# One S5 input chunk and one output-gate chunk share the K tiles on four accumulators

## The chip, the cores and the metric

The kernel runs on one core of a Trainium2 chip. The metric is the device time of one execution in microseconds (us); the median of three runs of the kernel before is 1253.27 us (1252.76 to 1253.33).

## What is computed

One layer of a hybrid block on 272 positions (16 learned meta tokens ahead of 256 tokens) of width 2048, in fp32, cut to what matters here:

```
xn   = rmsnorm(h)                                   # 272 x 2048
q, f, i, g, u = split(xn @ w_in)                    # 5 blocks of 1024 columns
o_hg = hgrn2(q, f, i)  -> per-head rms norm * gain * silu(g)
o_s5 = s5(u)           -> gelu, GLU with w_glu, rms norm
h    = h + concat(o_hg, o_s5) @ w_out
h    = h + conv_ffn(rmsnorm(h))                     # three matrices of 2048 x 5632
out  = rmsnorm(h[16:])
```

`hgrn2` is a gated linear recurrence of 8 heads with a 128x128 state, worked in chunks of 64 positions. `s5` is a diagonal complex state space of 64 groups of 16 channels with 64 states each. The output gate `g` is needed only when a head's output is put together.

## The kernel before, in words

**Matmuls.** Every projection works with fp32 split in two parts: the weights into `whi` (rounded, a ScalarE cast, L160) and `wlo` (the rest, a VectorE subtraction, L82 called by `wsplit`), the activations likewise into `xh` and `xl`. `mm3` issues three matmuls for each tile: high by high (L184), low activations by high weights (L185), high activations by low weights (L186). Weights come in units of 1 MB, that is 8 K tiles (128 rows each) of 256 columns; `wsplit` works them in two halves of 4 K tiles. A half gives 2 column blocks x 4 K tiles x 3 = 24 matmuls. Three buffers of `whi`, three of `wlo` and three raw units are in rotation, so a cast waits for the PE to finish the half three before it.

**Chunks.** `chunk` computes 256 columns of a projection in two PSUM accumulators from 2 units, 96 matmuls. u, f and i chunks are 272 positions wide, q and g chunks 258 (the last 258 positions suffice). The string `ORDER` lists what is written out one after the other: `u0` to `u3` are the S5 input chunks (`do_u`), `h0` to `h3` the f, q and i chunks of two heads each with the recurrence of these heads (`do_h`), `g0` to `g3` the output-gate chunks (`do_g`, then `hg_g` applies silu on ScalarE into `sg` and writes the gate `gs` on VectorE). Then follow the GLU of the S5 half (`gh` in the traces), the output projection (`mh`, `ml` are its activations) and the feed-forward.

**PSUM.** The eight banks are: `pmm`, 3 buffers for accumulators (`acc`); `pbu` 2; `py` 1; `psc` 1; `ptp` 1. A chunk holds two of the three `pmm` buffers until its results are read out, so the next chunk can begin on the third.

**Who sets the order.** The engines' instruction queues run in order. What comes after what on each queue is chosen at build time by a scheduler from priorities (`pri`, a lower number goes first) and its own estimates of durations; the source order is not the queue order.

**Around the start.** While the first chunks run, VectorE also normalises the 16 K tiles of the input (`xn`, L91; `xl`, L82) and works out the S5 coefficients. GpSimd (POOL) raises the S5 poles to powers, a long chain of small products on `pw` and `pt` that starts from a VectorE result (L86). VectorE copies the powers into `ew` (L472) when the chain is through; `cpc` (coefficients, from the scratch tile `sca`) and `W` (the decay weights of the scan) follow. `gs` lies in the same SBUF buffer as `sca`, a pool with one buffer for that tag. `early` holds two raw units loaded ahead of everything else, with part of their `wlo` made by POOL.

**At the end of this stage.** The last head pair's outputs are squared (`sq`), summed per head by the PE (`hps`), VectorE makes the 8 reciprocal roots (`rhv` to `rhy`, `hr`), the PE spreads them over 128 rows (`bps`, L854), VectorE multiplies (`oT`), and `mh`/`ml` of the 8 heads feed the output projection. The same is done for the S5 half (`ssum`, `s5s`, `rfv` to `rfy`, `ysb`), behind the GLU.

Of the kernel before, what the change touches and what calls it, by code (L numbers as in the profile page):

```python
# [9 lines left out]
F32 = mybir.dt.float32  # L10
# [8 lines left out]
T = SEQ + NM  # L19
# [10 lines left out]
T0 = NM - 2  # L30
# [3 lines left out]
NQ = T - T0  # L34
EPS = 1e-6
FLOOR = 1e-6
ORDER = "u0 h0 u1 h1 u2 h2 u3 h3 g0 g1 g2 g3"
U0 = 16
NWARM = 8
NWARM2 = 10  # L40
# [30 lines left out]
def hymba_kernel(ctx: ExitStack, tc: tile.TileContext, x, meta, lb_logits, norm_mix, w_in, hg_norm,  # L71
# [6 lines left out]
    def fact(dst, src, func=AF.Identity, **kw):  # L78
        act.activation(out=dst, in_=src, func=func, **kw)  # L79
# [10 lines left out]
    def stt(dst, a, s, b, op0, op1, **kw):  # L90
        dve.scalar_tensor_tensor(out=dst, in0=a, scalar=s, in1=b, op0=op0, op1=op1, **kw)  # L91
# [41 lines left out]
    def wload(src, parts=1):  # L133
        raw = wrp.tile([128, 2, 1024], F32, tag="raw", name="raw")
        if parts == 2:
            for a in range(2):
                sp.dma_start(out=raw[:, a].rearrange("p (a n) -> p a n", n=src.shape[2]), in_=src[:, 4 * a:4 * a + 4])
            return raw
        sp.dma_start(out=raw.rearrange("p a n -> p (a n)").rearrange("p (a n) -> p a n", n=src.shape[2]), in_=src)
        return raw  # L140

    early = []
    deps = []

    def wunit(src):
        with pri(-4):
            return wsplit(early.pop(0), (dve, pool), 2, deps.pop(0)) if early else wsplit(wload(src))

    def wsplit(raw, eng=(dve, dve), parts=1, dep=None):
        res = []  # L150
        n = 1024 // parts
        for hf in range(2):
            hi = wsp.tile([128, 1024], F32R, tag="whi", name="whi")
            lo = wsp.tile([128, 1024], F32R, tag="wlo", name="wlo")
            if dep is not None and dep[hf] is not None:

                act.copy(out=hi[:, 0:1], in_=dep[hf])
            for i in range(parts):
                c = slice(i * n, (i + 1) * n)
                act.copy(out=hi[:, c], in_=raw[:, hf, c])  # L160
                tt(lo[:, c], raw[:, hf, c], hi[:, c].bitcast(F32), SUB, eng[max(hf, i)])
            res.append((hi, lo))
        return res

    def colunit(w, k, c):
        return w[k * 1024:(k + 1) * 1024, c * 256:(c + 1) * 256].rearrange("(a p) n -> p a n", p=128)

    wpri = [1]

    def mm3(accs, units, rhs, n0, n1):  # L170

        last = len(units) - 1
        for ui, (u, k0) in enumerate(units):
            for hf, (hi, lo) in enumerate(u):
                for m in range(2):
                    for k in range(4):
                        kt = k0 + hf * 4 + k
                        lh = hi[:, k * 256 + m * 128:k * 256 + m * 128 + 128]
                        ll = lo[:, k * 256 + m * 128:k * 256 + m * 128 + 128]
                        first = ui == 0 and hf == 0 and k == 0  # L180
                        end = ui == last and hf == 1 and k == 3
                        xh, xl = rhs(kt)
                        with pri(wpri[0]):
                            pe.matmul(accs[m], lh, xh[:, n0:n1], start=first, stop=False)  # L184
                            pe.matmul(accs[m], lh, xl[:, n0:n1], start=False, stop=False)  # L185
                            pe.matmul(accs[m], ll, xh[:, n0:n1], start=False, stop=end)  # L186

    xh = xnp.tile([128, KD, T], F32R, tag="xh", name="xh")
    xl = xnp.tile([128, KD, T], F32R, tag="xl", name="xl")
# [8 lines left out]
    pmm = pmms.enter_context(tc.tile_pool(name="pmm", bufs=3, space=PSUM))  # L198
# [3 lines left out]
    psc = pa.enter_context(tc.tile_pool(name="psc", bufs=1, space=PSUM))  # L202
# [42 lines left out]
    sp.dma_start(out=crow, in_=conv_w.rearrange("o w (r c) -> (o w r) c", c=128).rearrange("(a p) c -> p a c", p=66))  # L245
    sp.dma_start(out=misc, in_=c_misc)
    sp.dma_start(out=masks, in_=c_masks.rearrange("p (l n) -> p l n", n=64))
    early.append(wload(colunit(w_in, 1, U0)))
    junk = xin.tile([128, D], mybir.dt.bfloat16, name="junk")
    junk2 = xin.tile([128, D], mybir.dt.bfloat16, name="junk2")  # L250

# [91 lines left out]
    def st(nm, p=prm, tag=None):  # L343
        return p.tile([128, NP], F32, tag=tag or nm, name=nm)
# [59 lines left out]
    xr, den, zr, zi, tz = st("xr"), st("den"), st("zr"), st("zi"), st("tz")  # L404
# [99 lines left out]
    k0 = [s5p.tile([128, 128], F32, name=f"k0{i}") for i in range(2)]  # L504
# [53 lines left out]
    def s5_u(j, ps):  # L558
        pv = ps.rearrange("p (k s) -> p s k", s=2)
        act.copy(out=ysb[:, j], in_=pv)  # L560

    def s5_split(j):
        R = s5w.tile([128, 2, TH], F32, tag="R", name="R")
        for q in range(4):
            h = 64 * (q % 2)
            sp.dma_start(out=R[h:h + 64, q // 2], in_=ysb[32 * q:32 * q + 32, j])
        return (R,)
# [104 lines left out]
    def hg_g(h0, accs):  # L672
        sg = hgp.tile([128, 2, NQ], F32, tag="sg", name="sg")
        for m in range(2):
            fact(sg[:, m], accs[m], AF.Sigmoid)
            stt(gs[:, h0 + m], accs[m], vcol[:, V_HG + h0 + m:V_HG + h0 + m + 1], sg[:, m], MUL, MUL)
# [83 lines left out]
    def chunk(w, c, n0=0):  # L760
        units = [(wunit(colunit(w, k, c)), k * 8) for k in range(2)]
        accs = [pmm.tile([128, T - n0], F32, tag="mm", name="acc") for _ in range(2)]
        mm3(accs, units, lambda kt: (xh[:, kt], xl[:, kt]), n0, T)
        return accs


    def do_u(c):
        accs = chunk(w_in, 16 + c)
        with pri(-3):
            for m in range(2):  # L770
                s5_u(2 * c + m, accs[m])
        for m in range(2):
            s5_tile(2 * c + m, *s5_split(2 * c + m), *s5_b(2 * c + m))
# [20 lines left out]
            hg_g(2 * c, accs)  # L794

    for o in ORDER.split():
        {"u": do_u, "h": do_h, "g": do_g}[o[0]](int(o[1]))

    s5ws.close()
    tls = ExitStack()  # L800
# [15 lines left out]
    for c in range(4):  # L816
        u = [(wunit(colunit(w_glu, 0, c)), 0)]
        accs = [pmm.tile([128, NQ], F32, tag="mm", name="acc") for _ in range(2)]
        mm3(accs, u, lambda kt: (gh[:, kt], gl[:, kt]), 0, NQ)
        with pri(-3):  # L820
            for m in range(2):
                j = 2 * c + m
                sg = tlp.tile([128, NQ], F32, tag="sq", name="sgl", bufs=3)
                fact(sg, accs[m], AF.Sigmoid, bias=vcol[:, V_BG + j:V_BG + j + 1])
                yv = ysb[:, j, :, K0:TH]
                tt(yv, yv, sp_view(sg), MUL)
                sq = ssum if j == 0 else tlp.tile([128, NQ], F32, tag="sq", name="sq", bufs=3)
                fact(sp_view(sq), yv, AF.Square)
                if j:
                    tt(ssum, ssum, sq, ADD)  # L830
# [30 lines left out]
    for c in range(8):  # L861
        u = [(wunit(colunit(w_out, 0, c)), 0)]
        accs = [pmm.tile([128, NQ], F32, tag="mm", name="acc") for _ in range(2)]
        mm3(accs, u, mixr, 0, NQ)
        with pri(-3):
            for m in range(2):
                tt(hT[:, 2 * c + m], hT[:, 2 * c + m], accs[m], ADD)
# [23 lines left out]
    for c in range(8):  # L891
        u = [(wunit(colunit(w_out, 1, c)), 8)]
        accs = [pmm.tile([128, NQ], F32, tag="mm", name="acc") for _ in range(2)]
        mm3(accs, u, mixr, 0, NQ)
        for m in range(2):
            kt = 2 * c + m
            g = vcol[:, V_FFN + kt:V_FFN + kt + 1]
# [20 lines left out]
    for c in range(FF // 256):  # L918
        accs = [pf.tile([128, NQ], F32, tag="f", name="ga") for _ in range(2)]
# [12 lines left out]
        accs = [pf.tile([128, NQ], F32, tag="f", name="ua") for _ in range(2)]  # L932
# [15 lines left out]
    for t in range(2):  # L948
        for n in range(4):
            for k in range(4):  # L950
                kt = n * 4 + k
# [20 lines left out]
    for j in range(KF - NT):  # L972
        a = act_split(j)
        u = wunit(w_down[j * 128:(j + 1) * 128, :].rearrange("p (a n) -> p a n", a=2))
# [72 lines left out]
```

## Time and profile before

| | |
|---|---|
| median of three runs | 1253.27 us |
| the profiled execution, device time | 1252.36 us |
| its span | 1250.6 us |
| PE (matmuls) busy | 1226.9 us, 98%, 9299 instructions |
| VectorE (DVE) busy | 873.7 us, 70% |
| ScalarE (ACT) busy | 601.2 us, 48% |
| GpSimd (POOL) busy | 117.0 us, 9% |
| mean granted TensorE clock | 0.994 |
| moved by DMA | 210.82 MB, mean 169 GB/s |

The profile comes from one execution; between its span and its device time lie 1.8 us. Engines are PE, PEld (weight loads, which overlap PE), DVE, ACT, POOL. A row of the timeline gives the start in us, the duration, the engine, the line, the operation, what is written and read, and in brackets how long the engine sat idle before it and whom it waited for. A row of the waits gives the waiting instruction, the releaser, the sum in us, the count and the longest. A row of the windows view gives the length of a stretch, the busy time and instruction count of PE, PEld, DVE, ACT and POOL, the granted clock, the DMA share and GB/s. A row of groups gives a count, the busy time, the mean in ns and the idle time ahead.

### The profile page before, as it was taken

What the parts mean: (1) busy time and instruction counts of PE and PEld (TensorE: products, weight loads), DVE (VectorE), ACT (ScalarE), POOL (GpSimd) and SP (SyncE); (2) the same over time, 40 slices, a digit from 0 to 9 for tenths busy, and PEclk for the clock granted to TensorE, in tenths of its full rate; (3) what the DMA queues carried; (4) which work ended last, traced back from release to release, by engine and by line L of the source; (5) the groups of instructions that cost most, each with busy time, mean ns of one, the idle gap of its engine ahead of it and who ended that gap; (6) DMA issues with size and microseconds to landing.
All of it is one profiled execution on the core that took longest, in us unless ns stands there. A gap on an engine that the chain in (4) does not pass through costs nothing.

```text
span 1250.6 us, 22795 instructions
## 1 busy us (share of the span) xinstructions
PE 1226.9 (98%) x9299; PEld 1151.9 (92%) x9299; DVE 873.7 (70%) x1516; ACT 601.2 (48%) x1042; POOL 117.0 (9%) x165
## 2 busy tenths in 40 slices
PE   7989999999999999999999999999999999999997
PEld 6979898989989999999999999999999988888886
DVE  8989999999748867765665656656656645554554
ACT  5646767574545446343433433433434434444454
POOL 5483132221000000000000000000000000000000
PEclk9989999999999999999999999999999999999999
DMA  8533344243444565565556555555555545555552
GB/s 256 147 122 113 105 144 136 86 134 127 144 135 136 169 201 172 167 203 179 192 172 199 171 196 173 193 178 187 184 181 191 210 166 198 202 188 187 197 205 98
DMA packets 176298, 210.82 MB, mean 169 GB/s; under 512 B 14773, under 2 KB 168880, under 8 KB 170416
## 3 DMA queue, kind: packets, MB, share of 16 engines
q1 hardware_dynamic: 175871, 209.26, 51.1%
q8 instruction: 73, 1.20, 0.4%
q14 instruction: 34, 0.27, 0.1%
q0 software_dynamic: 320, 0.09, 0.0%
HBM read 206.12 MB, written 2.10 MB: 166 GB/s over the span
## 4 chain that ended last, share of the span: by engine, by line
PE 92%; DVE 3%; POOL 2%; issue 1%; DMA 1%; ACT 0%; SPq 0%; DVEq 0%; ACTq 0%; POOLq 0%
PE acc L186 9%; PE acc L184 8%; PE acc L185 8%; PE ua L185 7%; PE ua L184 7%; PE ga L184 7%; PE ua L186 7%; PE ga L186 7%; PE ga L185 7%; PE d L970 6%; PE d L969 6%; PE d L968 6%; PE lps L713 1%; PE bu L600 1%; DVE xn L91 1%
## 5 line engine op out<-in xcount | busy, mean ns | idle before, releaser
L82 DVE TENSOR_TENSOR wlo<-raw,whi 128x1024 fp32r<-128x1024 f32 (+1 forms) x376 | 461.4, 1227 | 320.8 <-ACT whi L160 271.2
L160 ACT CAST whi<-raw 128x1024 fp32r<-128x1024 f32 (+1 forms) x382 | 397.8, 1042 | 519.9 <-PE ga L185 158.3
L184 PE MATMUL ga<-fh,whi 128*128 128x258 f32 x704 | 199.0, 283 | 0.5 <-DVE a L82 0.5
L186 PE MATMUL ga<-fh,wlo 128*128 128x258 f32 x704 | 198.5, 282 | 0.0
L185 PE MATMUL ua<-fl,whi 128*128 128x256 f32 x704 | 198.4, 282 | 0.0
L185 PE MATMUL ga<-fl,whi 128*128 128x258 f32 x704 | 198.1, 281 | 0.0
L186 PE MATMUL ua<-fh,wlo 128*128 128x256 f32 x704 | 197.9, 281 | 0.0
L184 PE MATMUL ua<-fh,whi 128*128 128x256 f32 x704 | 197.9, 281 | 0.0
L186 PE MATMUL acc<-xh,wlo 128*128 128x272 f32 (+1 forms) x640 | 186.7, 294 | 5.0 <-DVE wlo L82 5.0
L185 PE MATMUL acc<-xl,whi 128*128 128x272 f32 (+1 forms) x640 | 186.1, 292 | 3.9 <-DVE xl L82 3.9
L184 PE MATMUL acc<-xh,whi 128*128 128x272 f32 (+1 forms) x640 | 186.4, 294 | 0.4 <-ACT PP L79 0.4
L184 PEld LDWEIGHTS ga<-fh,whi 128*128 128x128 f32 x704 | 133.0, 189 | 0.7 <-DVE a L82 0.7
L185 PEld LDWEIGHTS ga<-fl,whi 128*128 128x128 f32 x704 | 133.5, 190 | 0.0
L184 PEld LDWEIGHTS ua<-fh,whi 128*128 128x128 f32 x704 | 133.1, 189 | 0.0
L186 PEld LDWEIGHTS ua<-fh,wlo 128*128 128x128 f32 x704 | 132.9, 189 | 0.0
L185 PEld LDWEIGHTS ua<-fl,whi 128*128 128x128 f32 x704 | 132.8, 189 | 0.0
L186 PEld LDWEIGHTS ga<-fh,wlo 128*128 128x128 f32 x704 | 132.6, 189 | 0.0
L186 PEld LDWEIGHTS acc<-xh,wlo 128*128 128x128 f32 x640 | 121.4, 190 | 9.4 <-DVE wlo L82 5.6
L185 PEld LDWEIGHTS acc<-xl,whi 128*128 128x128 f32 x640 | 121.6, 190 | 7.5 <-DVE xl L82 4.8
L968 PE MATMUL d<-whi,ah 128*128 128x512 f32 x328 | 127.7, 389 | 0.0
L969 PE MATMUL d<-whi,al 128*128 128x512 f32 x328 | 127.6, 389 | 0.0
L184 PEld LDWEIGHTS acc<-xh,whi 128*128 128x128 f32 x640 | 121.1, 190 | 4.1 <-issue 2.0
(381 smaller groups left out, 1868.1 us busy)
## 6 DMA issues: line engine op xcount, KB each, us to landing
raw<-in_w_ffn_gate SPq DMA_DIRECT2D x44, 1024.0 KB, 5.1
raw<-in_w_ffn_up SPq DMA_DIRECT2D x44, 1024.0 KB, 5.1
raw<-in_w_ffn_down SPq DMA_DIRECT2D x44, 1024.0 KB, 4.8
raw<-in_w_in SPq DMA_DIRECT2D x39, 1024.0 KB, 5.2
raw<-in_w_out SPq DMA_DIRECT2D x16, 1024.0 KB, 5.8
raw<-in_w_glu SPq DMA_DIRECT2D x4, 1024.0 KB, 5.2
x<-in_x SPq DMA_DIRECT2D x4, 512.0 KB, 5.7
out<-ob SPq DMA_DIRECT2D x8, 256.0 KB, 2.7
```

The lines of the kernel that those rows point to most:

```text
L82: eng.tensor_tensor(out=dst, in0=a, in1=b, op=op)
L91: dve.scalar_tensor_tensor(out=dst, in0=a, scalar=s, in1=b, op0=op0, op1=op1, **kw)
L160: act.copy(out=hi[:, c], in_=raw[:, hf, c])
L184: pe.matmul(accs[m], lh, xh[:, n0:n1], start=first, stop=False)
L185: pe.matmul(accs[m], lh, xl[:, n0:n1], start=False, stop=False)
L186: pe.matmul(accs[m], ll, xh[:, n0:n1], start=False, stop=end)
L600: return pe.matmul(bus[i][:, ri], bt[h, 2 * ri + q0 // 2], R[h, q0 // 2], start=True, stop=True)
L713: pe.matmul(ps[:, i], lhs[i], qf[:, 64 * i:64 * (i + 1)], start=True, stop=True)
L968: pe.matmul(dps[t][n], ah[:, tk], hi, start=False, stop=False, skip_group_check=True)
L969: pe.matmul(dps[t][n], al[:, tk], hi, start=False, stop=False, skip_group_check=True)
L970: pe.matmul(dps[t][n], ah[:, tk], lo, start=False, stop=end, skip_group_check=True)
```

## The change

`do_ug` takes the place of `u0` and of `g0`. The first u chunk and the first g chunk are computed together on four accumulators: half a unit of u (24 matmuls), half a unit of g, half a unit of u, and so on through the 16 K tiles. The four accumulators are all three `pmm` buffers and the one `psc` buffer; `gacc` takes the first `pmm` buffer and `psc`. `mm3` gets a `part` that picks the half of a unit. The second of the two early units is now the first g unit, not the second u unit. Then `do_u` goes on with the S5 work, and `hg_g` writes the gate of the first two heads. `ORDER` loses `g0`; `g1 g2 g3` stay at the end. The number of matmuls is the same.

```diff
-ORDER = "u0 h0 u1 h1 u2 h2 u3 h3 g0 g1 g2 g3"
+ORDER = "ug0 h0 u1 h1 u2 h2 u3 h3 g1 g2 g3"
...
-    def mm3(accs, units, rhs, n0, n1):
+    def mm3(accs, units, rhs, n0, n1, part=None):
 
         last = len(units) - 1
-        for ui, (u, k0) in enumerate(units):
+        for ui, (u, k0) in enumerate(units) if part is None else ((part[0], units[part[0]]),):
             for hf, (hi, lo) in enumerate(u):
+                if part is not None and hf != part[1]:
+                    continue
...
-    early.append(wload(colunit(w_in, 1, U0)))
+    early.append(wload(colunit(w_in, 0, 12)))
...
-    def do_u(c):
-        accs = chunk(w_in, 16 + c)
+    def do_ug(c):
+
+        gacc = [pmm.tile([128, NQ], F32, tag="mm", name="acc"), psc.tile([128, NQ], F32, tag="sc", name="acc")]
+        accs = [pmm.tile([128, T], F32, tag="mm", name="acc") for _ in range(2)]
+        xr = lambda kt: (xh[:, kt], xl[:, kt])
+        uu, gu = [None, None], [None, None]
+        for k in range(2):
+            uu[k] = (wunit(colunit(w_in, k, 16 + c)), k * 8)
+            gu[k] = (wunit(colunit(w_in, k, 12 + c)), k * 8)
+            for hf in range(2):
+                mm3(accs, uu, xr, 0, T, part=(k, hf))
+                mm3(gacc, gu, xr, T0, T, part=(k, hf))
+        do_u(c, accs)
+        with pri(-3):
+            hg_g(2 * c, gacc)
+
+    def do_u(c, accs=None):
+        accs = accs or chunk(w_in, 16 + c)
...
-        {"u": do_u, "h": do_h, "g": do_g}[o[0]](int(o[1]))
+        {"u": do_u, "h": do_h, "g": do_g, "ug": do_ug}[o.rstrip("0123456789")](int(o[-1]))
```

How the queues move, at three places. Line numbers of the changed kernel are higher by 2 up to the new function and by 18 behind it.

On PE, the first half of u and the start of the first half of g in the changed kernel (272 wide is u, 258 wide is g):

```order
L188 MATMUL acc<-xh,wlo 128x272
L186 MATMUL acc<-xh,whi 128x272 x2
L186 MATMUL acc<-xh,whi 128x258
L187 MATMUL acc<-xl,whi 128x258
L186 MATMUL acc<-xh,whi 128x258
L187 MATMUL acc<-xl,whi 128x258
L187 MATMUL acc<-xl,whi 128x272
L188 MATMUL acc<-xh,wlo 128x272
```

The matmuls of the two chunks do alternate; in the kernel before all 96 of u stand here without one 258 wide.

On DVE, the queue around the copies of the powers. Before:

```order
L82 TENSOR_TENSOR PP<-PP 128x272
L472 COPY ew<-pw 128x32 x3
L82 TENSOR_TENSOR wlo<-raw,whi 128x1024
L91 SCALAR_TENSOR_TENSOR cpc<-sca 128x32x16
L82 TENSOR_TENSOR qh<-q,PP 128x256
```

Now:

```order
L82 TENSOR_TENSOR sca<-scb,zar 128x512
L474 COPY ew<-pw 128x32 x3
L82 TENSOR_TENSOR wlo<-raw,whi 128x1024
L91 SCALAR_TENSOR_TENSOR cpc<-sca 128x32x16
L91 SCALAR_TENSOR_TENSOR W<-W,pw,tmp 128x2x17 x2
L91 SCALAR_TENSOR_TENSOR gs<-acc,vcol,sg 128x258 x2
L82 TENSOR_TENSOR wlo<-raw,whi 128x1024
L91 SCALAR_TENSOR_TENSOR q<-acc,lbc,sg 128x258 x2
```

The gate `gs` of the first two heads, which reads the g accumulators, stands behind the copies, behind the last reader of `sca` and behind two `W`; the read-out of q (`q<-acc,lbc,sg`) stands behind `gs`, where before it stood ahead of the copies. Ahead of the last VectorE instruction that the POOL chain starts from (L86 `pw`) eight 1024-wide `wlo` now stand where six stood.

On DVE, the reciprocal roots of the last heads at the end of the stage. Before:

```order
L82 TENSOR_TENSOR wlo<-raw,whi 128x1024
L82 TENSOR_TENSOR hr_5309<-rhy,hr_5309 8x258
L82 TENSOR_TENSOR ssum<-ssum,sq 128x258
L82 TENSOR_TENSOR ysb<-ysb,sgl 128x2x129
L82 TENSOR_TENSOR wlo<-raw,whi 128x1024
```

Now:

```order
L82 TENSOR_TENSOR wlo<-raw,whi 128x1024
L82 TENSOR_TENSOR ssum<-ssum,sq 128x258
L82 TENSOR_TENSOR ysb<-ysb,sgl 128x2x129
L82 TENSOR_TENSOR hr_5309<-rhy,hr_5309 8x258
L82 TENSOR_TENSOR ssum<-ssum,sq 128x258
L82 TENSOR_TENSOR oT<-oT,bps 128x258
L82 TENSOR_TENSOR ml<-oT,mh 128x258
L88 TENSOR_SCALAR rfv<-s5s 128x258
```

Counted in halves of units from the start of the program, the nearest `wlo` ahead of `hr` is that of half 87 before, and the PE is still in half 86 when it comes to the first `bps` (L854, now L872). Now it is that of half 91, and on PE the first `bps` stands directly behind the last matmul of half 88, the last of the GLU. From `hr` to the `ml` of the last head DVE has 46 instructions.

## The prediction

> **What bounds the kernel now.** The busy times of the page come first:
>
> ```profile
> PE 1226.9 (98%) x9299; PEld 1151.9 (92%) x9299; DVE 873.7 (70%) x1516; ACT 601.2 (48%) x1042; POOL 117.0 (9%) x165
> ```
>
> PE sets the time nearly everywhere, and the change keeps the number of matmuls. So it can act only through PE's idle time and PE's clock. Where that idle time lies, the waits of PE in the first 100 us and the windows around them tell:
>
> ```profile
> PE acc L186 <- DVE wlo L82: 5.0, 3, 3.6
> PE acc L185 <- DVE xl L82: 3.9, 3, 1.9
> PE dps L685 <- DVE q L91: 0.6, 1, 0.6
> ...
> 18.86:64.39 45.53, 40.76 (x324) 39.15 (x322) 43.06 (x125) 28.30 (x57) 23.44 (x37) 1.00 0.59 170
> 64.39:77.40 13.01, 11.40 (x88) 10.73 (x86) 13.01 (x20) 3.43 (x4) 13.01 (x18) 1.00 0.26 82
> 77.40:80.97 3.57, 0.00 (x0) 0.00 (x0) 2.04 (x6) 0.51 (x3) 3.57 (x6) 0.79 0.00 0
> 80.97:89.72 8.75, 8.75 (x49) 8.25 (x50) 7.85 (x16) 6.70 (x19) 5.75 (x11) 0.50 0.59 183
> 100.00:320.00 220.00, 220.00 (x1975) 200.99 (x1975) 212.15 (x456) 141.85 (x392) 55.65 (x64) 1.00 0.40 122
> ```
>
> The reader sees three losses. The first two windows hold 58.54 us with 52.16 us of matmuls, so 6.4 us of short waits. Then PE stands for 3.57 us. Then it runs 8.75 us at a granted 0.50, which costs half of that, 4.4 us. From 100 to 320 us PE has no gap. What ends the 3.57 us:
>
> ```profile
> 51.56 0.17 DVE L86 TENSOR_SCALAR pw<-pw 128x32 f32<-128x32 f32 x1
> ...
> 51.59 0.30 POOL L82 TENSOR_TENSOR pt<-pw 128x64 f32<-128x64 f32 x1 [11.06 <-DVE pw L82]
> 79.26 0.22 POOL L88 TENSOR_SCALAR pw<-pw 128x32 f32<-128x32 f32 x1
> ...
> 72.21 1.05 ACT L160 CAST whi<-raw 128x1024 fp32r<-128x1024 f32 x1 [0.46 <-PE acc L185]
> ...
> 78.94 0.86 DVE L472 COPY ew<-pw 128x32 f32<-128x32 f32 x3 [1.43 <-POOL pw L82]
> 79.70 1.21 DVE L82 TENSOR_TENSOR wlo<-raw,whi 128x1024 fp32r<-128x1024 f32 x1
> 80.84 0.80 DVE L91 SCALAR_TENSOR_TENSOR cpc<-sca 128x512 f32<-128x512 f32 x1
> 84.12 0.47 DVE L91 SCALAR_TENSOR_TENSOR W<-W,pw,tmp 128x34 f32<-128x34 f32 x2
> ...
> 80.97 0.60 PE L186 MATMUL acc<-xh,wlo 128*128 128x272 f32 x1 [3.61 <-DVE wlo L82]
> ```
>
> DVE hands `pw` to POOL at 51.6; POOL works on it for 27.9 us to 79.48; DVE stands at `ew` for it, and the `wlo` behind `ew`, whose cast was done at 73.3, runs only at 79.70. PE waits for that `wlo`. A long POOL chain sets this point, not the weights.
>
> **The middle, term by term.** The diff only doubles up two chunks; what counts is where `gs` now stands on DVE: behind `ew`, `wlo`, `cpc` and two `W`. `gs` is what empties the g accumulators, one of which is a `pmm` buffer; q, whose read-out stands behind `gs`, holds the other two. So u, g, f and q can be computed, and the first matmul of the i chunk must wait for `gs`.
>
> *When POOL is through.* Two more `wlo` stand ahead of the L86 `pw`. One costs 1.14 us from start to start (79.70 to 80.84): 2.3 us. DVE is nearly full there (43.06 of 45.53 us), so little is absorbed; I take 1.8 to 2.3. POOL then ends at 81.3 to 81.8.
>
> *When `gs` is written.* Behind POOL's end: the last `ew` copy, `wlo` 1.14 and `cpc` 0.73 (80.84 to the next start), to about 2.1; then `W`, which needs ScalarE's `tmp` on POOL's next power:
>
> ```profile
> 81.86 0.54 ACT L79 ACTIVATE tmp<-W,pw 128x34 f32<-128x34 f32 x2 [1.51 <-POOL pw L82]
> ```
>
> `tmp` is through 2.9 us after POOL's 79.48, two `W` add about 0.5, the first `gs` 0.48 (its row is below): 4.0 us. The first `gs` is written at 85.3 to 85.8; I take 85.4.
>
> *What PE has done by then.* u and g (192 matmuls) with f and q (192) are the same amount as u, f, q and i before, less 28 columns of 272 in one chunk: 52.16 us of work from 18.86. Before, PE resumed behind that work at 80.97; now at 85.4. **+4.4 us.** The bounds are 0, if `W` and `gs` meet no wait and DVE absorbs the two `wlo`, and +6.
>
> The early `xl` waits (3.9 us) shrink, since 24 matmuls of g stand between two halves of u; I take 1.7 us of them gone. That is worth nothing here: PE only stops earlier, near 75.7, and waits some 9.7 us instead of 3.57.
>
> *The clock.* A mean of 0.79 in the 3.57 us window means 1.5 us at 0.50: the clock fell near 79.5, 2.1 us into the idle time. It was back at 89.72, 10.24 us later:
>
> ```profile
> 89.72:100.00 10.28, 10.28 (x95) 9.91 (x95) 8.96 (x20) 7.25 (x24) 3.55 (x7) 1.00 0.46 136
> ```
>  With a wait of 9.7 us it would fall near 77.8 and come back near 88.0; of that, 2.6 us would lie behind the restart and cost 1.3 instead of 4.4: up to −3.1. If the low clock lasts longer where most of it is idle, nothing is gained. I take **−1.5 us**. [...]
>
> The first work of the S5 scan and of head 0 moves by about the 2 us of POOL's lateness; behind 100 us DVE has 8 us of slack in 220, and PE never waits. 0, up to +1.
>
> **The tail, term by term.** One g chunk fewer stands at the end: 96 matmuls of 0.12 us (389.85 to 389.97 below), 11.5 us of PE work that covered the last heads' output. The rows of before:
>
> ```profile
> 400.00:420.00 20.00, 19.60 (x143) 17.85 (x142) 18.24 (x41) 10.03 (x19) 0.00 (x0) 1.00 0.37 108
> ...
> 386.35 0.42 DVE L82 TENSOR_TENSOR hr<-rhy,hr 8x258 fp32r<-8x258 f32 x1
> 388.10 1.23 DVE L82 TENSOR_TENSOR wlo<-raw,whi 128x1024 fp32r<-128x1024 f32 x1 [0.54 <-ACT whi L160]
> 389.24 0.42 DVE L82 TENSOR_TENSOR ssum<-ssum,sq 128x258 f32<-128x258 f32 x1
> 389.57 0.42 DVE L82 TENSOR_TENSOR ysb<-ysb,sgl 128x258 f32<-128x258 f32 x1
> 389.91 0.42 DVE L82 TENSOR_TENSOR oT<-oT,bps 128x258 f32<-128x258 f32 x1
> ...
> 387.01 1.05 ACT L160 CAST whi<-raw 128x1024 fp32r<-128x1024 f32 x1 [0.97 <-PE acc L185]
> ...
> L854 PE MATMUL bps<-hr,hsel x8: 379/382/384, 389.3 to 406.6; 40*128 40x258 f32 x8
> ...
> 389.85 0.28 PE L184 MATMUL acc<-gh,whi 128*128 128x258 f32 x1
> 389.97 0.28 PE L185 MATMUL acc<-gh,whi 128*128 128x258 f32 x1
> ...
> L82 DVE TENSOR_TENSOR wlo<-raw,whi 128x1024 fp32r<-128x1024 f32 x36 | 44.1, 1224 | 25.5 <-ACT whi L160 25.3
> L91 DVE SCALAR_TENSOR_TENSOR gs<-acc,vcol,sg 128x258 f32<-128x258 f32 x8 | 3.8, 481 | 0.4 <-ACT sg L79 0.4
> L82 DVE TENSOR_TENSOR ml<-oT,mh 128x258 fp32r<-128x258 f32 x8 | 3.4, 422 | 0.0
> L91 DVE SCALAR_TENSOR_TENSOR ysb<-ysb,vcol,rfy 128x258 f32<-128x258 f32 x8 | 3.3, 483 | 0.0
> ```
>
> Before, `hr` is done at 386.77 and PE comes to the first `bps` at 389.3: 2.5 us of slack, and the 20 us behind 400 hold 0.4 us of PE idle time.
>
> *The first `bps`.* Now it stands on PE right behind half 88, and `hr` on DVE behind the `wlo` of half 91. That half needs the `whi` buffer of half 88, so its cast starts when PE is at the last matmuls of half 88, and the chain cast, `wlo`, `ssum`, `ysb`, `hr` follows while PE stands. Its length is in the rows: from the cast at 387.01 to 389.91, the start behind `ysb`, 2.90 us, and 0.42 for `hr`: **3.3 us** of wait. This doesn't depend on how early the roots were begun.
>
> *Behind it.* PE has 66 matmuls for K tiles of the heads done (66 x 0.12 = 7.9) and `bps` and `s5s`, 9 at 0.2 to 0.38 (2.7 at the middle): 10.6 us, until it needs the last head's `ml`. DVE has the 46 instructions from `hr` to that `ml`: one `wlo` 1.14, 8 `ysb` at about 0.40 and 37 others at 0.34 from start to start (389.57 to 389.91): 1.1 + 3.2 + 12.6 = 16.9 us, since the S5 `ml` and `ysb` stand ahead of the last `ml`. PE waits the difference, 6.3 us, in pieces at the `bps`. With the 3.3, and less the 0.4 of before: **+9.2 us**. The bounds are +3 (only the first wait, with DVE's rows going on while it lasts) and +11.5, the whole cover that left.
>
> **Sum.** +4.4 − 1.5 + 9.2 = +12.1 on the profiled execution's 1252.36, 1264.5; that execution lies 0.9 us under the median of 1253.27, well inside what a difference can be told by. I forecast **1264 us**.
>
> **Rivals.**
>
> *The clock falls a second time, in the tail.* The clock fell once PE had stood 2.1 us, and the first `bps` waits 3.3. For: exactly that row. Against: shorter gaps (1.9 us at `xl`) left it at 1.00, and the span between is thin. 10.24 us at 0.50, some 8 of them behind the wait, take 4 us of PE work, of which DVE's lateness hides about half: **1267 us**.
>
> *The tail stays covered.* DVE may run the roots and the S5 rows early enough that only small waits are left, the chain of half 91 hidden by a longer stretch of matmuls than the queue shows. For: DVE idles 25.3 us for casts between 320 and 440. Against: the buffer rotation above forces the cast behind half 88. Then only the middle counts: 1252.36 + 4.4 − 1.5 = **1255 us**.
>
> *It gets faster.* The interleave takes PE's early waits away, and if `gs` is done before PE has finished q near 75.7, PE never stands: 3.57, 4.4 of clock and 1.7 of `xl` waits are won, 9.7 us: **1243 us** with the tail covered, 1252 with it uncovered. The mechanism is the read-out of g; it decides at POOL's end. `gs` is due 4.0 us behind that, so POOL would have to end by 71.7, 7.8 us ahead of its 79.48 and in spite of a later start. Its 27.9 us were measured beside a busy DVE, and a quieter DVE could shorten them; but nothing in the rows removes DVE work there. [...]
>
> *It doesn't do what it says.* If the four accumulators were worked chunk after chunk, the g chunk would merely have moved; the PE queue shows u and g halves alternating, so I give this little. PE's sum and so the time would be that of before, **1253 us**, if both covers held.
>
> **How the numbers follow.** Chances: my forecast 0.55 (its own range 1258 to 1270), second clock fall 0.14, tail covered 0.14, faster 0.12, no change 0.05. This kernel's runs can't tell less than about 0.2%, 2.5 us. Slower by more than that are the first two and most of the third: 0.80; within it, 0.08; faster 0.12. The range runs from 1253, the low end of a covered tail and the case of no change, to 1271, which takes in the second clock fall and the upper bound of the tail; it leaves out the faster case and the far ends.
>
> **What would show it.** In the middle: a PE wait of some 9 to 10 us ahead of the first i matmul, put down to DVE `gs`, ending near 85.4, POOL's chain starting near 53.5, and `xl` waits under 3 us. In the tail: a wait over 3 us at the first `bps`, more at the later ones, and DVE without gaps from `hr` on. I am wrong if `gs` ends before 80 us, if DVE's rows behind `hr` are already run when PE comes to `bps`, or if the low clock lasts well behind 90 us.

## The result, and the profile after

The changed kernel takes 1262.13 us (median of 4 runs, 1261.24 to 1263.25); the kernel before took 1253.28 us in the same comparison (4 runs, 1252.76 to 1253.33). The ratio is 1.0077, with a 95% interval of 1.0065 to 1.0089: slower by 8.85 us; this is the figure to go by. The profiled execution has a span of 1261.5 us (1250.6 before) and a device time of 1263.25 us, so that this one execution lies 10.9 us behind the one that the prediction was summed on; the two profiled executions are 2 us further apart than the medians. The mean granted clock is 0.987 (0.994 before).

The page of the changed kernel, busy times and the granted clock in 40 slices:

```profile
PE 1229.7 (97%) x9299; PEld 1154.9 (92%) x9299; DVE 872.6 (69%) x1516; ACT 604.9 (48%) x1043; POOL 120.8 (10%) x165
PEclk9979999999998899999999999999999999999999
```

The matmuls are the same 9299. The clock shows a dip in the third slice, as before the change, and a second one in the slices from 378 to 441 us: that is the end of the stage. The waits of PE, up to 110 us and from 300 to 440 us, agree on the two places:

```profile
PE acc L186 <- DVE gs L91: 11.5, 1, 11.5
PE acc L187 <- DVE xl L82: 1.1, 2, 0.6
...
PE bps L872 <- DVE hr L82: 3.4, 1, 3.4
PE acc L188 <- DVE wlo L82: 2.0, 1, 2.0
PE acc L187 <- DVE ml L82: 0.7, 1, 0.7
```

**The middle.** The timeline: the first product of POOL's chain and its last power, DVE from the copies on, and PE's restart:

```profile
52.98 0.31 POOL L82 TENSOR_TENSOR pt<-pw 128x64 f32<-128x64 f32 x1 [11.93 <-DVE pw L82]
...
80.50 0.26 POOL L88 TENSOR_SCALAR pw<-pw 128x32 f32<-128x32 f32 x1
...
80.19 1.15 DVE L474 COPY ew<-pw 128x32 f32<-128x32 f32 x3 [7.21 <-POOL pw L82]
81.24 1.21 DVE L82 TENSOR_TENSOR wlo<-raw,whi 128x1024 fp32r<-128x1024 f32 x1
82.38 0.80 DVE L91 SCALAR_TENSOR_TENSOR cpc<-sca 128x512 f32<-128x512 f32 x1
83.10 0.47 DVE L91 SCALAR_TENSOR_TENSOR W<-W,pw,tmp 128x34 f32<-128x34 f32 x2
83.50 0.87 DVE L91 SCALAR_TENSOR_TENSOR gs<-acc,vcol,sg 128x258 f32<-128x258 f32 x2
...
82.67 0.54 ACT L79 ACTIVATE tmp<-W,pw 128x34 f32<-128x34 f32 x2 [0.78 <-POOL pw L82]
...
84.12 0.56 PE L186 MATMUL acc<-xh,whi 128*128 128x272 f32 x1 [11.48 <-DVE gs L91]
```

The order is the one that the prediction followed: POOL's chain, `ew`, `wlo`, `cpc`, `W`, `gs`, and PE behind `gs`. The windows around the standing PE:

```profile
19.03:72.63 53.60, 52.09 (x419) 50.60 (x417) 53.12 (x140) 34.16 (x63) 30.94 (x42) 1.00 0.58 172
72.62:84.12 11.50, 0.02 (x2) 0.03 (x1) 4.19 (x10) 1.96 (x7) 11.26 (x23) 0.64 0.16 53
84.12:89.52 5.40, 5.40 (x32) 5.15 (x36) 4.44 (x13) 3.63 (x14) 2.45 (x6) 0.50 0.52 180
```

PE was busy for 52.1 us in 53.60 us instead of 58.54, stopped at 72.62 and stood for 11.5 us. The same two stretches, the matmuls into `acc` alone (before, then now), and the first 100 us of both kernels:

```profile
18.86:77.40 58.54, 49.66 (x366) 46.25 (x366) 0.95 (x2) 2.91 (x8) 1.00 0.51 150
19.03:72.62 53.59, 50.43 (x384) 47.86 (x384) 0.00 (x0) 2.91 (x8) 1.00 0.58 172
...
0.00:100.00 100.00, 85.76 (x640) 81.22 (x641) 87.97 (x227) 58.09 (x134) 59.34 (x98) 0.95 0.57 172
0.00:100.00 100.00, 83.89 (x639) 80.16 (x640) 82.81 (x220) 59.31 (x133) 58.54 (x98) 0.93 0.57 174
```

When it stops, PE has now begun 384 matmuls into `acc`, all of u, g, f and q; before it had begun 366 (and eight `dps`, small matmuls of the recurrence, that now come later). By 100 us both kernels have begun the same number of matmuls, 640 and 639. It restarts 3.15 us later than before (84.12 against 80.97), but only 5.40 us of its work then falls under the granted 0.50 (8.75 us before), since most of the low clock lies in the standing time. At half of the time under it, an estimate from the granted 0.50, that is 2.7 instead of 4.4 us. The 272 wide matmuls of the kernel before start 0.226 us apart at 0.50 (81.37 to 83.86 us) and 0.125 at 1.00 (89.74 to 90.99), which makes it 45%: 2.4 instead of 3.9.

**The tail.** The timeline around the first `bps` and the windows behind it:

```profile
395.35 1.04 ACT L160 CAST whi<-raw 128x1024 fp32r<-128x1024 f32 x1 [0.78 <-PE acc L187]
396.43 1.23 DVE L82 TENSOR_TENSOR wlo<-raw,whi 128x1024 fp32r<-128x1024 f32 x1 [0.21 <-ACT whi L160]
398.36 0.42 DVE L82 TENSOR_TENSOR hr<-rhy,hr 8x258 fp32r<-8x258 f32 x1
398.83 0.38 PE L872 MATMUL bps<-hr,hsel 40*128 40x258 f32 x1 [3.40 <-DVE hr L82]
...
405.86 0.42 DVE L82 TENSOR_TENSOR oT<-oT,bps 128x258 f32<-128x258 f32 x1 [0.84 <-PE bps L872]
407.97 0.42 DVE L82 TENSOR_TENSOR oT<-oT,bps 128x258 f32<-128x258 f32 x1 [0.88 <-PE bps L872]
...
412.69 1.21 DVE L82 TENSOR_TENSOR wlo<-raw,whi 128x1024 fp32r<-128x1024 f32 x1
413.96 0.58 PE L188 MATMUL acc<-mh,wlo 128*128 128x258 f32 x1 [1.98 <-DVE wlo L82]
```

```profile
396.72:400.14 3.42, 1.23 (x4) 0.66 (x4) 2.88 (x6) 1.48 (x4) 0.00 (x0) 1.00 0.81 275
400.14:406.96 6.82, 6.82 (x26) 5.79 (x26) 5.65 (x16) 1.22 (x3) 0.00 (x0) 0.50 0.00 1
410.38:413.80 3.42, 1.60 (x9) 1.12 (x9) 3.42 (x7) 2.84 (x8) 0.00 (x0) 1.00 0.00 0
413.80:420.62 6.82, 5.92 (x26) 5.63 (x26) 5.77 (x17) 1.84 (x5) 0.00 (x0) 0.50 0.48 156
```

PE waits 3.4 us at the first `bps`, and once it runs again the clock is at 0.50 for 6.8 us; meanwhile DVE waits for PE (the two `oT` rows); then PE waits 2.0 and 0.7 us more, and the clock is at 0.50 for another 6.8 us. Before, the windows behind 400 us stood at 1.00.

**Where the 10.9 us are.** The last matmul of the GLU starts at 396.3 us before and at 395.2 now. Two of the eight `bps` (0.3 us each) stand ahead of it before, none now; without them the changed kernel is 0.6 us ahead at that point. From there to the first matmul of the feed-forward PE takes 97.1 us before and 109.2 now; less the two `bps` that is 11.5 us more. Behind it nothing changes (757.1 us in both). So the whole loss is in the tail: 6.1 us of waits, less the 0.4 of before, and 5.8 us that are left for two stretches of low clock (an upper bound for these from the windows is half of 6.82 and half of 5.92, 6.4 us; the 258 wide matmuls of the changed kernel start 0.215 us apart at 0.50, from 416.95 to 418.67 us, and 0.12 at 1.00, from 420.90 to 421.62, which makes it 5.6).

### The profile page after: what moved, and what is told of

It is laid out like the page before. It is cut to its first block, busy times and chain, and to the rows that moved or that the text cites. A ratio compares the mean times of both kernels' runs of the same rounds, so it can differ in the third digit from the quotient of the medians.

```text
span 1261.5 us, 22794 instructions
## 1 busy us (share of the span) xinstructions
PE 1229.7 (97%) x9299; PEld 1154.9 (92%) x9299; DVE 872.6 (69%) x1516; ACT 604.9 (48%) x1043; POOL 120.8 (10%) x165
## 4 chain that ended last, share of the span: by engine, by line
PE 85%; DVE 9%; POOL 2%; DMA 1%; ACT 1%; issue 1%; SPq 0%; DVEq 0%; ACTq 0%; POOLq 0%
PE acc L186 7%; PE acc L187 7%; PE acc L188 7%; PE ua L187 7%; PE ua L186 7%; PE ga L186 7%; PE ua L188 7%; PE ga L188 7%; PE ga L187 7%; PE d L986 6%; PE d L988 6%; PE d L987 6%; DVE wlo L82 2%; PE lps L715 1%; DVE W L91 1%
## 5 line engine op out<-in xcount | busy, mean ns | idle before, releaser
L186 PE MATMUL acc<-xh,whi 128*128 128x272 f32 (+1 forms) x640 | 186.0, 293 | 11.9 <-DVE gs L91 11.5
```

## The experiments

All are compared with the kernel before on the same chip. Two numbers are read from each trace. The *lead* is the start of the GLU's last matmul less the start of `hr` on DVE: how early the roots are there. The *tail cost* is the time from that matmul to the first matmul of the feed-forward, less the 97.1 us of before, with 0.3 us allowed for each `bps` that stands on the other side of the GLU's end. All runs at once:

| kernel | hr starts | GLU's last matmul | lead | tail cost | low clock in the tail | ratio to before |
|---|---|---|---|---|---|---|
| before | 386.3 | 396.3 | +10.0 | 0 | none | 1 |
| after | 398.4 | 395.2 | −3.2 | 11.5 | 2 x 6.8 us | 1.0077 |
| before, g0 ahead of h3 | 391.2 | 397.3 | +6.1 | 0.6 | none | 1.0013 |
| before, 9 steps in the roots | 402.6 | 394.5 | −8.1 | 15.2 | 20.5 us | 1.0105 |
| after, 1 step | 391.5 | 395.2 | +3.7 | 7.0 | 6.8 us | 1.0041 |
| after, no step | 390.1 | 396.7 | +6.6 | 0.6 | none | 0.9998 |
| after, gate in its own buffer | 396.0 | 395.9 | −0.1 | 9.6 | 2 x 3.4 us | 1.0071 |
| after, h3 ahead of u3 | 379.7 | 404.9 | +25.2 | −1.6 | none (6.8 us ahead of the GLU's end) | 1.0048 |
| u0 and g0 one after the other | 398.3 | 400.9 | +2.6 | 7.4 | 3.4 and 6.8 us | 1.0104 |
| before, with zero matmuls | 391.9 | 404.8 | +12.8 | −0.3 | none | 1.0044 |
| before, product on DVE | 384.5 | 394.5 | +10.0 | 0 | none | 0.9990 |
| after, three edits | 389.8 | 393.6 | +3.8 | 9.2 | 6.8 and 3.4 us | 1.0066 |

**The lost cover alone.** One edit in the kernel before takes the same 96 matmuls away from behind the last heads, but puts them ahead of `h3` and not at the start:

```diff
-ORDER = "u0 h0 u1 h1 u2 h2 u3 h3 g0 g1 g2 g3"
+ORDER = "u0 h0 u1 h1 u2 h2 u3 g0 h3 g1 g2 g3"
```

> The kernel before with the first gate chunk moved to just ahead of h3 and nothing else: no interleave, the start as before, and behind h3 the same matmuls as in the changed kernel (g1, g2, g3 and the GLU). Theory of lost cover (the prediction's tail term): the 11.5 us of matmuls that are gone behind h3 cost about 9 to 10 us, time about 1262. Rival, that the tail costs this only where the last head pair's recurrence itself ends late or where the reciprocal roots stand late in VectorE's queue: here they stand one half earlier, so the wait at the first bps is under 1 us and the time 1253 to 1256.

Measured: 1254.31 us against 1252.60, ratio 1.0013 (1.0003 to 1.0022). So the theory that the loss is the lost amount of cover falls, and with it the bound that the prediction had taken from it. The rival's range (1253 to 1256) holds the time, and PE doesn't wait at the first `bps`. The groups by tile (count, durations, first and last start): the squares' sums of the changed kernel, whose `hr` starts at 398.4 us, then the sums and the roots of this one:

```profile
L861 PE MATMUL hps<-sq,misc x16: 381/381/385, 375.4 to 384.5; 128*8 128x258 f32 x16
```

```profile
L843 PE MATMUL hps<-sq,misc x16: 381/381/386, 368.5 to 377.5; 128*8 128x258 f32 x16
L82 DVE TENSOR_TENSOR hr<-rhy,hr x1: 419/419/419, 391.2 to 391.2; 8x258 fp32r<-8x258 f32 x1
```

The same number of matmuls is left behind `h3`, and yet the last sum is there 7.0 us earlier. The recurrence of the last heads takes 54.8 us here (from its first `dps` at 310.6 to its last `ops` at 365.4) against 62.4 us in the changed kernel (309.5 to 371.9) and 62.7 in the kernel before. Between `u3` and `h3` stand 11.5 us of matmuls, in which DVE can do the S5 work of `u3` before the recurrence asks for it; that last part is argued from the order, not measured apart.

**When the roots come.** The lead can be moved by the number of Newton steps in the heads' reciprocal roots, without touching the order of the chunks (2.7 to 3.5 us a step from 9 to 3 and from 3 to 1, by the starts of `hr` in the table). A step is three small DVE instructions, so DVE's work in the tail changes along with the lead. The kernel with no step takes the first guess as the root, so part of the computation is left out; with one step the root is coarser.

```diff
-        hrs = rsqrt(hgp, hps, [8, NQ], 1.0 / 128, "rh", tags=("iv", "qm", "v"))
+        hrs = rsqrt(hgp, hps, [8, NQ], 1.0 / 128, "rh", tags=("iv", "qm", "v"), steps=9)
```

with `for _ in range(steps)` in place of 3 in `rsqrt`: 9 in the kernel before, 1 and 0 in the changed one.

> The kernel before with nine Newton steps instead of three in the reciprocal roots of the last heads: 18 more small VectorE instructions between the head sums and hr, every chunk where it was, the matmuls behind h3 unchanged. New theory (what counts is when hr is ready against the end of the GLU's matmuls): hr comes 8 to 10 us later, at 394 to 396, about when the GLU's matmuls end, and the tail costs 8 to 12 us as in the run with gs in its own buffer: 1261 to 1265. Theory of lost cover: the matmuls behind h3 are all there, 10 us of slack for 7 us of work, so 0 to 2 us: 1253 to 1255.

> The changed kernel with one Newton step instead of three in these roots (the output is then less exact in the recurrent heads; two thirds of the iteration are left out): six VectorE instructions fewer ahead of hr. New theory: hr at 391 to 393 instead of 398.4, 2 to 4 us ahead of the end of the GLU's matmuls instead of 3 behind; no wait at the first bps, tail cost 3 to 6 us instead of 11, time 1255 to 1258. Theory of lost cover: the waits only move to the later bps and the last ml, 1260 to 1262.

> The same with no Newton step (the iteration is left out altogether): hr at 388 to 390, 5 to 7 us ahead of the end of the GLU's matmuls. New theory: like the run with g0 ahead of h3, tail cost 0 to 2 us, time 1252 to 1254, although the start with its 11.5 us wait is that of the changed kernel; this would also show that the start costs no more than about 1 us. Theory of lost cover: 1258 to 1261.

Measured: with 9 steps the kernel before takes 1266.77 us against 1253.53, ratio 1.0105 (1.0090 to 1.0121), more than any theory had said, with `hr` at 402.6 us where 394 to 396 were expected. With one step the changed kernel takes 1258.19 us, 1.0041 (1.0027 to 1.0055), just above the new theory's range and well under the old one's; with none 1252.94 us, 0.9998 (0.9989 to 1.0007). Nothing was taken from or given to the matmuls behind `h3` in these three. The waits of the kernel before with 9 steps, and the window behind:

```profile
PE s5s L833 <- DVE ssum L82: 4.4, 1, 4.4
PE bps L854 <- DVE hr L82: 3.2, 1, 3.2
```

```profile
399.69:420.17 20.48, 16.34 (x57) 13.06 (x57) 18.23 (x48) 7.44 (x17) 0.00 (x0) 0.50 0.03 5
```

It has all the cover and pays 15.2 us in the tail: 7.6 us in these two waits, and 20.5 us at a granted 0.50, in which PE is busy for 16.3. The changed kernel with no step, its longest wait up to 110 us, then a window of the tail:

```profile
PE acc L186 <- DVE gs L91: 11.5, 1, 11.5
```

```profile
385.00:425.00 40.00, 39.19 (x288) 35.73 (x288) 34.29 (x74) 20.50 (x37) 0.00 (x0) 1.00 0.41 128
```

The 11.5 us at `gs` are still there, the tail is whole, and the time is that of the kernel before. This says two things: the new start costs about nothing, and the loss of the changed kernel is all in the tail and goes when the roots come early. Whether it goes by the lead or by the nine DVE instructions that are gone can't be told apart here; in the run with `g0` ahead of `h3`, which has them all, it goes as well.

**The wait for the gate.** In the changed kernel `gs` gets its own SBUF buffer, so that it need not wait for the last reader of `sca`:

```diff
-    gs = ogp.tile([128, NH, NQ], F32, tag="gs", name="gs")
+    gs = ogp.tile([128, NH, NQ], F32, tag="gsown", name="gs")
```

> The changed kernel with gs in a buffer of its own, so that it need not wait for the last reader of sca; in VectorE's queue gs then stands ahead of the ew copies. Theory (the release of the g accumulators sets the restart): the wait of 11.5 us on gs is gone; what is left is VectorE standing at ew for POOL until about 80.5, so a wait of 3 to 5 us at a wlo and perhaps one more for q, together 5 to 8 us; time 1256 to 1260. Rival, that POOL's chain holds PE whatever happens to gs: PE again stands 10 us or more, time within 1 us of 1262.

Measured: 1261.27 us, 1.0071 (1.0056 to 1.0086): a miss for the theory's time, which the rival had right, though PE stands for 7.5 us and not 10. `gs` is now written at 47.4 and 49.7 us, and the 11.5 us are gone from the list; PE's waits, up to 110 us and behind it:

```profile
PE dps L687 <- DVE q L91: 7.5, 1, 7.5
...
PE acc L187 <- DVE ml L82: 2.7, 2, 1.8
PE bps L872 <- DVE oT L82: 1.7, 3, 0.7
PE acc L186 <- DVE xT L82: 1.7, 1, 1.7
```

q, the next to be read out, stands behind the same copies of POOL's powers, and PE restarts at 84.2 us, where the changed kernel does. The buffer was the name of the wait; the POOL chain sets its end. The shorter wait did buy work: up to 84.2 us PE has begun 533 matmuls, 25 more than the changed kernel. By 360 us that is gone (2948 against 2954), though PE is busy for all of the 220 us from 100 to 320. So a PE without gaps didn't begin its matmuls at one rate there, 2415 from 84.2 to 360 us against 2446 in the changed kernel; DVE is busy for 210.66 of these 220 us, but that it sets the pace is not shown. The tail pays 9.6 us with `hr` waiting only 0.3 us at the first `bps`: what is late then is the rest of DVE's queue.

**The last two chunks exchanged.** In the changed kernel `h3` goes ahead of `u3`:

```diff
-ORDER = "ug0 h0 u1 h1 u2 h2 u3 h3 g1 g2 g3"
+ORDER = "ug0 h0 u1 h1 u2 h2 h3 u3 g1 g2 g3"
```

> The changed kernel with u3 written out behind h3, so that again four chunks stand between h3 and the GLU; the start is that of the changed kernel. Theory of lost cover: the tail's 9 to 11 us come back, the wait of 11.5 us on gs stays, time 1251 to 1254. Rival, that the recurrence of the last heads is late because VectorE is full and not for lack of matmuls behind it: hr is late again, time 1258 to 1263.

Measured: 1258.63 us, 1.0048 (1.0033 to 1.0063). The time lies in the rival's range, but not by its mechanism: `hr` is at 379.7 us, no `bps` waits, and the clock behind 385 us is at 1.00. But the S5 half is now the late one: PE waits at the start of the GLU, and the clock falls there.

```profile
PE acc L186 <- ACT gh L831: 3.9, 1, 3.9
```

```profile
374.77:381.59 6.82, 5.06 (x22) 4.91 (x23) 5.35 (x16) 2.88 (x9) 0.00 (x0) 0.50 0.07 22
```

The heads and the S5 half share DVE; whichever goes last is the chain that isn't covered.

**Without the interleave.** The kernel before, with the gate chunk at the same place in the program but behind `u0` and not mixed with it:

```diff
-ORDER = "u0 h0 u1 h1 u2 h2 u3 h3 g0 g1 g2 g3"
+ORDER = "u0 g0 h0 u1 h1 u2 h2 u3 h3 g1 g2 g3"
```

> The kernel before with the order u0 g0 h0 u1 h1 u2 h2 u3 h3 g1 g2 g3: the first gate chunk comes second as in the changed kernel, but the two go one after the other on two accumulators each, with three in rotation. If the interleave itself is worth nothing because only the release of the accumulators counts, the time is within 2 us of the changed kernel's 1262. If the shorter waits for xl (1.1 us against 3.9) and the earlier end of g count, it is 3 to 6 us longer, 1265 to 1268. The tail should be the changed kernel's in both.

Measured: 1265.12 us, 1.0104 (1.0089 to 1.0119). PE's waits up to 110 us:

```profile
PE acc L184 <- DVE gs L91: 7.2, 1, 7.2
PE acc L185 <- DVE xl L82: 3.5, 2, 1.8
```

The `xl` waits are near those of the kernel before (3.9 us); in the changed kernel they are 1.1. The GLU ends 5 us late here and on time there. So the interleave itself is worth about 3 us against the plain move (the two intervals just touch), as the second forecast had it; the move of the gate chunk is what costs. That the two tails would be alike did not hold: 7.4 us here, 11.5 there.

**The clock in the middle.** To price the low clock alone, 24 matmuls with a zero operand were put where the kernel before stands for 3.57 us:

```diff
                             pe.matmul(accs[m], lh, xl[:, n0:n1], start=False, stop=False)
+                            for _ in range(fill if ui == last and hf == 1 and m == 0 and k == 0 else 0):
+                                pe.matmul(accs[m], lh, zt[:, n0:n1], start=False, stop=False)
```

> The kernel before with 24 more matmuls by a block of zeros (they add zero to an accumulator) placed at the point of the 3.6 us wait for the wlo behind ew; 3.0 us of work that the wait covers. If the low clock behind the wait comes from PE standing still, the clock stays at 1.00 there. Then either all 4.4 us are won, 1248 to 1249, or, if what PE comes to next (ktp, ready near 84.2) was waiting to become the bound, only what lies behind 84.2: 2.7 us, 1250. If the clock falls anyway, or the zeros don't count as work, the time is that of before or up to 1 us more.

Measured: 1258.32 us, 1.0044 (1.0031 to 1.0056): a miss, and no price follows from it. The timeline of PE, and a window:

```profile
77.75 2.31 PE L187 MATMUL acc<-zt,whi 128*128 128x272 f32 x17
84.91 0.42 PE L554 MATMUL ktp<-cp,eb 128*32 128x32 f32 x4 [4.86 <-ACT cp L544]
```

```profile
77.75:82.62 4.87, 2.30 (x19) 2.08 (x17) 1.99 (x6) 0.51 (x3) 4.87 (x8) 1.00 0.00 0
```

17 of the 24 ran in the gap and the clock held up to 82.62 us. Then PE stood for 4.9 us at the next instruction in line, which needs ScalarE's `cp`, the clock fell in that wait, to 0.50 until 92.86 us, and the other 7 ran under it ahead of real work, in 1.75 us, 0.25 each, where the 17 start 0.13 apart. The whole loss lies ahead of the GLU's end; the tail is free.

**Work off the POOL chain.** The last two look for a better version. In the first, one of the two products in each doubling of `ew` goes from POOL to DVE, in the kernel before. In the second the changed kernel gets this, the gate's own buffer and shorter roots (ScalarE's square root, a reciprocal and one Newton step).

```diff
-        tt(et3[:, :, :, 0:n], ew[:, :, 0:2, 0:n], sb, MUL, pool)
+        tt(et3[:, :, :, 0:n], ew[:, :, 0:2, 0:n], sb, MUL)
```

> The kernel before with one of the two products of each doubling of ew (four multiplications) on VectorE instead of POOL; nothing else. If the length of POOL's chain sets the restart of PE and the wait's length sets the clock, POOL ends about 2 to 3 us earlier, the 3.6 us wait shrinks under 2.5 us or splits up, the clock stays at 1.00 and 3 to 6 us are won: 1247 to 1250. If VectorE, busy for 24.9 of these 27.9 us, only hands the delay on to other waits of over 3 us, the time is that of before, 1252 to 1255.

> The changed kernel with gs in a buffer of its own, the same product on VectorE, and the last heads' reciprocal roots from ScalarE's square root, a reciprocal and one Newton step, 6 VectorE instructions ahead of hr instead of 13. By the new theory of the tail hr is ready 3 us or more ahead of the end of the GLU's matmuls and the tail costs 0 to 5 us; in the middle the wait of 11.5 us splits into two of 3 to 4 us. 1248 to 1254. If the tail follows the matmuls behind h3 and not hr, it costs 9 us as before: 1257 to 1262.

Measured: the first takes 1251.64 us (11 runs) against 1252.64, ratio 0.9990 (0.9981 to 0.9998). The copies `ew` run at 75.5 instead of 78.9 us and the 3.61 us wait at 81 is gone, but a wait of 2.46 us for another `wlo` has come at 69.2, and a low clock behind it. The time lies between the two forecasts. It is the one version here that beats the kernel before, by 1.0 us with an interval that ends close to 1. The second takes 1260.64 us, 1.0066 (1.0052 to 1.0079): a miss. Its GLU ends 2.5 us ahead of the kernel before with the `bps` taken out, and `hr` is there at 389.8, but a lead of 3.8 us isn't enough: the tail costs 9.2 us. None of PE's waits there is for `hr`; they are for `xT` (2.3 us), `mh` (1.6) and `ml` (0.9), rows that come behind it.

## Why the prediction was right, and where not

The forecast was 1264 us with a range of 1253 to 1271, slower at 0.80; 1262.13 was measured. On the profiled execution's time the sum was +12.1, and +10.9 was found. The direction and the two places were rightly told. That the sum comes so near is luck in part: the middle was put 3.5 us too high (+2.9 for −0.6) and the tail 2.3 us too low (+9.2 for +11.5).

- **Middle, the restart (+4.4).** Measured +3.15. POOL began at 52.98 and not at 53.4 to 53.9, so its end came 0.5 us earlier than the 81.3 that was taken as the earliest; and from POOL's end to PE's restart went 3.4 us and not 4.0, since `W` at 83.10 follows `cpc` at once, and ScalarE's `tmp` (82.67) didn't hold it up. The mechanism and the order were as told: 11.5 us were seen where 9 to 10 were said, because PE stopped 3 us earlier than 75.7. The `xl` waits shrank by 2.8 and not 1.7 us, and the other short waits of the start went too: 6.4 us of them before, 1.5 in the 53.60 us now.
- **Middle, the clock (−1.5).** At half of the time under 0.50 it is −1.7, by the spacing of the matmuls −1.5, by the route described: low clock spent in standing time. It fell at 75.87 and came back at 89.52, 13.6 us and not 10.24.
- **The middle as a whole (+2.9).** By these two +1.45 would be left, but at the GLU's end the changed kernel is 0.6 us ahead. The step that failed here is "the same amount": the prediction took u, g, f and q to be the work that PE had done before when it stood. Before, PE had begun 366 of those 384 matmuls, so the changed kernel restarts later with 18 more behind it, 2.2 us at 0.12 each, and eight `dps` fewer (and the g chunk is 14 columns narrower than the i chunk that it stands for, not 28). By 100 us the two are level. What is left, half a microsecond, can't be told: the kernel before and its version with 9 steps are the same up to the roots, and end the GLU at 396.3 and 394.5 us, 1.3 us apart without the two `bps`.
- **The tail, first `bps` (3.3).** Measured 3.40, by the chain that was named: cast at 395.35, `wlo`, `ssum`, `ysb`, `hr`, PE. But the sentence that this "doesn't depend on how early the roots were begun" was wrong. With one Newton step `hr` stands at 391.5, ahead of half 91's `wlo`, and the first `bps` (394.44) doesn't wait. The place of `hr` in DVE's queue moved with the length of the roots; the queue that was read as given was a result of it.
- **The tail, behind it (6.3).** This is the step of the tail that failed. It set 10.6 us of PE work against 16.9 us of DVE work without gaps, and had PE wait the difference at the `bps`. None of the later `bps` waited. DVE's 46 rows took 20.4 us (398.36 to 418.73) with gaps of 0.18, 0.84, 0.88 and 0.28 us at the `oT` rows that wait for `bps`, the first three of them in or right behind the stretch in which PE ran at 0.50. PE waited 2.7 us, for a `wlo` and an `ml`, and 5.8 us went into two stretches at 0.50, for which the sum had no term.
- **The rival of a second clock fall (0.14, 1267 us).** Its mechanism happened, twice. What the prediction held against it, that gaps of 1.9 us had left the clock at 1.00, doesn't carry over: the wait of 1.85 us that left it at 1.00 in the kernel before was followed by 0.50 in the kernel with one product on DVE (last section).
- **What bounds the tail.** The upper bound of +11.5, "the whole cover that left", and the reading that the loss is that cover, fell with the first experiment: the same 96 matmuls taken away cost 0.6 us when `hr` came in time. The cost goes with the lead: at +6.1 and more the tail is free, at +3.8 and less it costs 7 to 15 us, with nothing seen in between. Within the costly runs the lead doesn't order the cost (9.2 us at +3.8, 7.4 at +2.6). In each of them PE's waits make up 3.1 to 8.2 us, less the 0.4 of before, and the rest, 3.2 to 7.0 us, goes with stretches at 0.50; none had the one without the other.
- **The other rivals.** "Gets faster" asked for POOL's end by 71.7; it was 80.8. "Stays covered" didn't happen here, but the changed kernel with no Newton step is that case, at 1252.94 us and not the 1255 that was worked out for it: again the middle's term. "Doesn't do what it says" is out: PE's early waits shrank as an interleave makes them shrink.

## What to carry to other kernels

When a block of matmuls is moved away from behind a chain, don't price the block; price the lead of the chain's last result over the point at which PE needs it, before and after. For the same block of 11.5 us the lead fell by 13.2 us in the changed kernel and by 3.9 us with `g0` ahead of `h3`, where the chain itself got shorter; and a lead of a few microseconds more or less separates nothing from 7 us. A wait in PE's list has a name and an end: giving `gs` its own buffer took the name away and left the end, which another engine's chain had set; look for what the next instruction in line would wait for.

## What the runs showed of the hardware

In these traces the granted clock changed on a grid. In the changed kernel and in the kernel before all changes between 1.00 and 0.50 up to 440 us lie at whole multiples of 3.41 us from each other. In the changed kernel they are 75.87, 89.52, 400.14, 406.96, 413.80 and 420.62 us (the window rows above end there, or, for 75.87, give it by the mean of 0.64 from 72.62 to 84.12): the low stretches last 4, 2 and 2 steps, and from 75.87 to 400.14 are 95.0. In the kernel before they are 79.48 and 89.72, 3 steps. In the other ten traces, looked at from 20 to 100 and from 385 to 425 us, each step of 3.41 us reads 1.00 or 0.50 as a whole, with an offset of its own in each trace. The kernel before and its version with 9 steps, which are the same up to the roots, fell at 79.48 and at 82.26 us, 2.78 apart, and stayed low for 10.24 and 6.82 us. Whether the spread of the 15 runs of the kernel before beside the Newton runs (mean clocks of 0.990 to 0.994, times of 1252.31 to 1254.28 us) comes from such offsets is not shown.

The falls go with the time that PE stood inside one step. The same wait for `xl` near the start shows it. The kernel before, its row and two steps of its grid:

```profile
28.61 0.39 PE L185 MATMUL acc<-xl,whi 128*128 128x272 f32 x1 [1.85 <-DVE xl L82]
```

```profile
24.86:28.28 3.42, 1.89 (x14) 1.56 (x12) 3.42 (x5) 1.44 (x4) 3.42 (x3) 1.00 0.11 37
28.28:31.69 3.41, 2.63 (x19) 2.41 (x20) 3.41 (x8) 1.91 (x4) 1.17 (x1) 1.00 0.69 210
```

The kernel with one product on DVE, the same wait and its steps:

```profile
28.78 0.39 PE L185 MATMUL acc<-xl,whi 128*128 128x272 f32 x1 [1.85 <-DVE xl L82]
```

```profile
25.83:29.24 3.41, 1.56 (x12) 1.34 (x11) 3.41 (x4) 0.64 (x2) 3.41 (x3) 1.00 0.00 1
29.24:32.66 3.42, 3.40 (x16) 3.04 (x15) 3.42 (x9) 2.25 (x5) 0.38 (x1) 0.50 0.89 286
```

Both wait 1.85 us. In the first a step ends within the wait, at 28.28: 1.53 us of standing fall into one step, 0.78 into the next, and the clock stays. In the second the whole wait falls into one step, and the next step runs at 0.50. From 20 to 100 and from 385 to 425 us, in all twelve traces, every step at 1.00 with 1.73 us of standing or more (22 steps) was followed by 0.50; of those with 1.18 to 1.64 us 5 were followed by 0.50 and 11 by 1.00; none with less was followed by 0.50. In every step at 0.50 that was followed by 1.00 PE stood for 0.56 us or less; one to four such steps in a row came ahead of the return. So the same wait of 1.85 us was followed by a step at 0.50, with 3.40 us of PE's work in it, in one kernel and by none in the other; at the 45% above that step costs 1.5 us, an estimate.
